# Narrower first score tiles, and chunk-end gate sums with the indicator as the stationary operand, in a two-layer hybrid encoder on one Trainium2 core

## The chip, the cores and the metric

The kernel runs on one core of a Trainium2 chip. The core has a matrix engine (PE in the profile, with its weight loads listed apart as PEld), a vector engine (DVE), an activation engine (ACT), a general engine (POOL), and a queue engine (SP) that mostly starts DMA transfers. The metric is device time in microseconds for one execution. Before the change the median of three runs is 1642.15 us (1640.87 to 1643.2). Lower is better.

A matmul on PE has a stationary operand, which is loaded into the array first (a LDWEIGHTS record in the profile), and a moving operand that is streamed through it. In `nc.tensor.matmul(out, a, b)` the second argument is the stationary one and the third the moving one. Where the text says "128 columns" of a matmul, it means the columns of the moving operand.

## The reference, cut to what matters

```python
D_MODEL = 2048; SEQ = 512; DEPTH = 2; CHUNK = 64
GLA_HEADS = 4; GLA_DK = 128; GLA_DV = 256; ATT_HEADS = 8; ATT_HD = 128

def gla_chunk_causal(q, k, v, log_a):
    L = jnp.cumsum(log_a.reshape(B, nc, CHUNK, H, DK), axis=2)
    L_end = L[:, :, -1]                        # sum of the log gates of a chunk
    k_dec = kf * jnp.exp(L_end[:, :, None] - L)
    U = jnp.einsum('bnchk,bnchv->bnhkv', k_dec, vf)
    A = jnp.exp(L_end)                         # decay of the state over a chunk
    # S_c = A_c * S_{c-1} + U_c, every frame of chunk c reads S_c

def chunk_band_attention(q, k, v, rel_bias):
    # queries of chunk c attend to chunks c-8..c, plus a relative bias, softmax

def hybrid_layer(x, ...):
    z = rmsnorm(x, g_pre) @ w_in               # one projection, columns split into groups
    log_a = log_sigmoid(ga @ w_alpha + b_alpha) / 16
    o_gla = rmsnorm(gla_chunk_causal(gq, gk, gv, log_a)) * silu(gg)
    o_att = rmsnorm(chunk_band_attention(aq, ak, av, rel_bias)) * silu(ag)
    return x + rmsnorm(concatenate([o_gla, o_att]) @ w_out, g_post)
```

There are 512 tokens, so 8 chunks of 64 tokens, and 4 tiles of 128 tokens. A query tile i (128 tokens) attends to the keys 0 to 128(i+1), since 9 chunks reach back to the start of the sequence. `A` has one number for each layer, head, key feature and chunk: 4 x 128 x 8 per layer.

## The kernel before, in words

Nearly all the work is two large matrix products per layer (the input and the output projection), cut into blocks of 512 columns (`std_gemm`, line 340) and, for pairs of blocks, into seven products of halves in place of eight (`fast_gemm`, lines 416 and 426). Every operand is split into a high and a low float32 part (`float32r`, the type `F32R` in the code), and three products of parts are accumulated: high by high, high by low, low by high. The weights come from HBM by SP's queue, ACT makes the high part (line 217), DVE the low part (line 222), and PE multiplies.

Everything else (norms, gates, attention, gated linear attention) is written as Python generators, "tasks". After each block of projection matmuls a pacing object advances the first tasks by a few steps, so that their instructions stand between those of the projection. The framework then orders the instructions of each engine by its own estimate of a timeline when the program is built; each engine executes its own list strictly in that order.

Two tasks are touched by the change.

- **Attention scores** (`Head.scores`, lines 863 to 888). For each head and query tile i three float32r matmuls (lines 871 to 873) give 128 queries by `n` keys in one PSUM tile, with the queries as stationary operand. `n` is `max(lk, 256)` with `lk = (i + 1) * P`, P = 128. For i = 0 that is 256 keys, though only the first 128 are read afterwards. 8 heads by 2 layers by 3 matmuls are 48 such matmuls.
- **Decay of the gates** (`forget_gate_decay`, from line 754). For each of four token tiles t, `ps_g` is the gate's projection (line 781), three activations and one DVE operation make the log gates `la` (128 tokens by 512 features), and they are split into `lah` and `lal`. `finish_tile` sums them: lines 769 and 770 are two float32r matmuls with the fixed matrix `later` as stationary operand, and line 772 makes the chunk sums. There, `la` itself (plain float32) is stationary, 128 by 128 for each head, and the moving operand is `chunk_ind`, two columns that hold 1/16 for the tokens of the first and the second chunk of the tile. The result stands with features on partitions, 2 columns per tile and head, 32 columns in all (`ps_end`). At the end one ACT instruction (line 803) writes `a_end`, the exponential of these 32 columns. `a_end` is read much later, when the states are accumulated (line 1101, first at 605.7 us), and the flag `fgate["done"]` lets the key block's evacuation begin.

A plain float32 matmul leaves two records in the profile, a float32r matmul one. Transposes (line 893) are matmuls of plain float32 with an identity as moving operand and leave one record.

Of the kernel before, what the change touches and what calls it, by code (L numbers as in the profile page):

```python
# [7 lines left out]
F32 = mybir.dt.float32  # L8
F32R = mybir.dt.float32r
BF16 = mybir.dt.bfloat16  # L10
AF = mybir.ActivationFunctionType
# [4 lines left out]
P = 128  # L16
# [4 lines left out]
NT = S // P  # L21
# [13 lines left out]
def hybrid_trunk(  # L35
# [13 lines left out]
    nc = tc.nc  # L49
    cpool = ctx.enter_context(tc.tile_pool(name="cpool", bufs=1))  # L50
# [15 lines left out]
    def nm(s):  # L66
        serial[0] += 1
        return f"{s}_{serial[0]}"

    def slot(tag, shape, dtype=F32):  # L70
        return slots.tile([P] + shape, dtype, tag=tag, name=nm(tag))
# [4 lines left out]
    def t2(shape=(512,), dtype=F32):  # L76
        return tmp.tile([P] + list(shape), dtype, tag="t2", name=nm("t2"))
# [7 lines left out]
    def sm(cols, tag="sm", bufs=None):  # L85
        return small.tile([P, cols], F32, tag=tag, name=nm(tag), **({"bufs": bufs} if bufs else {}))

    def aux():
        return ps_ax.tile([P, 512], F32, tag="ax", name=nm("ax"))
# [14 lines left out]
    def flat(t):  # L104
        return t.bitcast(F32).rearrange("p a b -> p (a b)")

    def split(hi, lo, src):
        nc.scalar.copy(hi, src)  # L108
        nc.vector.tensor_tensor(out=lo, in0=src, in1=hi.bitcast(F32), op=ALU.subtract)
# [9 lines left out]
    ident = cst[:, 0:P]  # L119
    chunk_ind = cst[:, 2 * P : 2 * P + 2]  # L120
    ones = cst[:, 2 * P + 2 : 3 * P + 2]
    mhalf = cpool.tile([P, 4], F32, tag="mhalf", name="mhalf")
    eps = cpool.tile([P, 1], F32, tag="eps", name="eps")
    later = cpool.tile([P, P], F32R, tag="later", name="later")

    CO = (0, 4, 1, 5, 2, 6, 3, 7)
    OO = (5, 4, 7, 6, 2, 3, 0, 1)
# [400 lines left out]
    def neg_inv_rms(l, t):  # L528
        return norm[l][:, 1, t : t + 1]

    def rms(l, t):
        return norm[l][:, 2, t : t + 1]
# [141 lines left out]
    nc.gpsimd.memset(mhalf, -0.5)  # L674
    nc.gpsimd.memset(eps, EPS)
    nc.vector.tensor_copy(later, cst[:, P : 2 * P])

    fg_weights = {}

# [26 lines left out]
    def layer(l):  # L706
# [22 lines left out]
        a_end = sm(32, "a_end", 2)  # L729
# [28 lines left out]
        def forget_gate_decay():  # L758
            fac = slot("g8", [2, 512], F32R)
            nc.sync.dma_start(flat(fac)[0:98], fac_d[l][0:98])  # L760
            wal, gaT = fac[0:98, 0, :], fac[0:98, 1, :]
            yield
            ps_end = aux()

            def finish_tile(t, la, lah, lal):
                if t % 2 == 0:
                    decay.append(slot(f"g{9 + t // 2}", [2, 512]))
                ps_d = aux()
                nc.tensor.matmul(ps_d, later, lah, start=True, stop=False)
                nc.tensor.matmul(ps_d, later, lal, start=False, stop=True)  # L770
                for h in range(4):
                    nc.tensor.matmul(
                        ps_end[:, h * 8 + 2 * t : h * 8 + 2 * t + 2], la[:, h * P : (h + 1) * P], chunk_ind,
                        start=True, stop=True,
                    )
                nc.scalar.activation(decay[t // 2][:, t % 2, :], ps_d, AF.Exp)

            pend = []
            for t in range(NT):
                ps_g = aux()  # L780
                nc.tensor.matmul(ps_g, gaT[:, t * P : (t + 1) * P], wal, start=True, stop=True)
                e = t2()
                nc.scalar.activation(e, ps_g, AF.Abs)
                nc.scalar.activation(e, e, AF.Exp, scale=-1.0)
                nc.scalar.activation(e, e, AF.Ln, bias=ones[:, 0:1])
                la = t2()
                nc.vector.scalar_tensor_tensor(
                    out=la, in0=ps_g, scalar=0.0, in1=e, op0=ALU.min, op1=ALU.subtract
                )
                yield  # L790
                lah, lal = t2(dtype=F32R), t2(dtype=F32R)
                split(lah, lal, la)
                yield
                yield
                pend.append((t, la, lah, lal))
                if t:
                    finish_tile(*pend.pop(0))
                    yield
            for _ in range(4):
                yield  # L800
            finish_tile(*pend.pop(0))
            yield
            nc.scalar.activation(a_end, ps_end[:, 0:32], AF.Exp)
            fgate["done"] = True
            yield

# [39 lines left out]
        def load_bias(n):  # L846
            if n >= 8:
                return
            b = tmp.tile([P, 512], F32, tag="bias", name=nm("bias"), bufs=2)
            src = rel[l, HEADS[n]]  # L850
            nc.sync.dma_start(b, bass.AP(tensor=src.tensor, offset=src.offset + 127, ap=[[639, P], [1, 512]]))
            nc.vector.memset(b[0:64, 448:512], MASKED)
            biases[HEADS[n]] = b
# [4 lines left out]
        class Head:  # L858
# [6 lines left out]

            def scores(self, i):
                lk = (i + 1) * P
                n = max(lk, 256)
                t = slice(i * P, (i + 1) * P)
                ps = aux()  # L870
                nc.tensor.matmul(ps[:, :n], self.qh[:, t], self.kh[:, :n], start=True, stop=False)  # L871
                nc.tensor.matmul(ps[:, :n], self.qh[:, t], self.kl[:, :n], start=False, stop=False)  # L872
                nc.tensor.matmul(ps[:, :n], self.ql[:, t], self.kh[:, :n], start=False, stop=True)  # L873
                pr = self.prob[i] = t2((lk,))
                nc.scalar.activation(pr, biases[self.hd][:, 512 - lk : 512], AF.Copy, scale=rms(l, i))
                nmx = sm(1)
                nc.vector.tensor_tensor_reduce(
                    out=pr, in0=ps[:, :lk], in1=pr, op0=ALU.add, op1=ALU.min,
                    scale=neg_inv_rms(l, i), scalar=-NEG, accum_out=nmx,
                )  # L880
                nc.scalar.activation(pr, pr, AF.Exp, bias=nmx, scale=-1.0, accum_out=self.lsum[:, i : i + 1])
                if i == 0:
                    self.el = sm(4)
                    nc.vector.scalar_tensor_tensor(
                        out=self.el, in0=self.lsum, scalar=EPS, in1=self.lsum, op0=ALU.mult, op1=ALU.mult
                    )
                    load_bias(HEADS.index(self.hd) + 2)
# [129 lines left out]

        until(lambda: 0 in heads_done)
        tasks.insert(0, forget_gate_decay())
        kdh, kdl, gqT = [], [], []  # L1020

# [378 lines left out]
```

## Time and profile before

| | |
|---|---|
| median of three runs | 1642.15 us (1640.87 to 1643.2) |
| the profiled execution | 1640.27 us, of which the span from first to last instruction is 1638.3 us |
| granted TensorE clock | 0.999 |
| PE busy | 1628.6 us (99% of the span), 9030 matmul records |
| DVE busy | 1227.9 us (75%) |
| ACT busy | 903.3 us (55%) |
| POOL busy | 161.9 us (10%) |
| DMA | 469.59 MB, mean 287 GB/s |

A matmul's duration in the profile is longer than the time that it costs, because matmuls overlap: the 512-column ones are listed with some 390 ns each but start every 0.227 us. What one costs is therefore read from the distance between starts, or from the chain of waits, whose pieces do not overlap. The page's busy shares do not tell it.

### The profile page before, as it was taken

Reading aid. Unit: us, or ns where it says so; the run is one execution under the profiler, and the core shown is the slowest. Engines: PE = TensorE matmul, PEld = TensorE weight load, DVE = VectorE, ACT = ScalarE, POOL = GpSimd, SP = SyncE. Lnnn points to the kernel's source line nnn. Section 1 sums busy time; section 2 is a strip of 40 time slices with the busy share of each in tenths; the row PEclk is TensorE's granted clock in tenths of the full one; section 3 lists DMA queues with packets and bytes.
Section 4 is the critical chain, followed back from the end, with each engine's and each line's share of the span. In section 5 each row is a group of like instructions: output and inputs, shape, how many; then the busy total and the mean of one; then the engine's idle time right before and its main releaser. Section 6 shows DMA issues by size and latency. Waiting matters only on the chain.

```text
span 1638.3 us, 24908 instructions
## 1 busy us (share of the span) xinstructions
PE 1628.6 (99%) x9030; PEld 1397.8 (85%) x9030; DVE 1227.9 (75%) x1583; ACT 903.3 (55%) x1514; POOL 161.9 (10%) x258
## 2 busy tenths in 40 slices
PE   9999999999999999999999999999999999999998
PEld 7888889999988877788888888899999888777886
DVE  7567776877877886778886676768778778766887
ACT  8444544556666644545784445445556766445543
POOL 1210000000101101310122000000001001013100
PEclk9999999999999999999999999999999999999999
DMA  9979786858858696898789697968588576968986
GB/s 374 362 281 327 274 316 228 298 184 312 288 185 291 209 376 235 300 365 314 279 297 385 238 327 270 322 219 302 190 307 281 196 275 231 358 225 331 369 306 238
DMA packets 150778, 469.59 MB, mean 287 GB/s; under 512 B 16428, under 2 KB 35892, under 8 KB 150656
## 3 DMA queue, kind: packets, MB, share of 16 engines
q1 hardware_dynamic: 128064, 389.69, 67.9%
q0 software_dynamic: 22016, 77.37, 12.1%
q8 instruction: 71, 1.16, 0.3%
q10 hardware_dynamic: 576, 0.95, 0.2%
q14 instruction: 51, 0.42, 0.1%
HBM read 395.83 MB, written 71.06 MB: 285 GB/s over the span
## 4 chain that ended last, share of the span: by engine, by line
PE 98%; DMA 1%; DVE 0%; issue 0%; ACT 0%; DVEq 0%; POOLq 0%
PE mm L426 46%; PE mm L340 21%; PE mm L416 20%; PE ax L910 2%; PE ax L1080 1%; PE ax L426 1%; PE ax L893 1%; PE ax L1114 1%; PE ax L741 1%; DMA t<-fg 1%; PE ax L873 1%; PE ax L872 1%; PE ax L871 1%; PE ax L1142 0%; PE ax L941 0%; PE ax L568 0%
## 5 line engine op out<-in xcount | busy, mean ns | idle before, releaser
L426 PE MATMUL mm<-wh,sa 128*128 128x512 f32 x1536 | 484.5, 391 | 0.1
L217 ACT CAST wh<-raw 128x1024 fp32r<-128x1024 f32 x255 | 268.7, 1055 | 252.6 <-PE mm L426 119.5
L222 DVE TENSOR_TENSOR wl<-raw,wh 128x1024 fp32r<-128x1024 f32 (+1 forms) x257 | 312.4, 1217 | 118.8 <-PE mm L426 37.2
L217 ACT CAST wh<-H 128x1024 fp32r<-128x1024 f32 x224 | 235.3, 1053 | 219.9 <-PE mm L426 117.6
L222 DVE TENSOR_TENSOR wl<-H,wh 128x1024 fp32r<-128x1024 f32 x224 | 273.3, 1222 | 109.0 <-PE mm L426 49.4
L426 PEld LDWEIGHTS mm<-wh,sa 128*128 128x128 f32 x1536 | 288.1, 188 | 61.6 <-issue 2.3
L426 PE MATMUL mm<-wl,sa 128*128 128x512 f32 x768 | 300.3, 391 | 0.0
L416 PE MATMUL mm<-sa,wh 128*128 128x256 f32 x1280 | 237.1, 285 | 0.0
L416 PEld LDWEIGHTS mm<-sa,wh 128*128 128x128 f32 x1280 | 199.9, 191 | 0.3
L426 PE MATMUL mm<-wh,a 128*128 128x512 f32 x576 | 186.5, 393 | 0.0
L416 PE MATMUL mm<-sa,wl 128*128 128x256 f32 x640 | 180.6, 283 | 0.0
L426 PEld LDWEIGHTS mm<-wl,sa 128*128 128x128 f32 x768 | 144.3, 188 | 29.1
L340 PE MATMUL mm<-wh,a 128*128 128x512 f32 x512 | 166.9, 393 | 0.0
L206 DVE TENSOR_TENSOR H<-H,raw 128x1024 f32<-128x1024 f32 x120 | 145.9, 1220 | 3.7 <-DMA raw<-in_w_dram 2.0
L464 POOL TENSOR_TENSOR sm<-sm,mhalf 128x4 f32<-128x4 f32 (+2 forms) x40 | 53.0, 1325 | 770.5 <-DVE sm L926 542.5
L426 PEld LDWEIGHTS mm<-wh,a 128*128 128x128 f32 x576 | 107.9, 188 | 23.1 <-issue 0.8
L416 PEld LDWEIGHTS mm<-sa,wl 128*128 128x128 f32 x640 | 122.3, 191 | 0.1
L340 PEld LDWEIGHTS mm<-wh,a 128*128 128x128 f32 x512 | 95.9, 188 | 21.2 <-ACT a L108 0.6
L426 PE MATMUL mm<-wl,a 128*128 128x512 f32 x288 | 113.4, 394 | 0.0
L340 PE MATMUL mm<-wl,a 128*128 128x512 f32 x256 | 100.3, 393 | 0.3 <-DVE wl L222 0.3
L416 PE MATMUL mm<-a,wh 128*128 128x256 f32 x512 | 94.7, 285 | 0.0
L340 PE MATMUL mm<-wh,sa 128*128 128x512 f32 x256 | 86.0, 394 | 0.0
(203 smaller groups left out, 2337.3 us busy)
## 6 DMA issues: line engine op xcount, KB each, us to landing
raw<-in_w_dram SPq DMA_DIRECT2D x319, 512.0 KB, 5.7
sa<-S SPq DMA_DIRECT2D x192, 512.0 KB, 4.8
H<-in_w_dram SPq DMA_DIRECT2D x56, 512.0 KB, 4.7
sa<-A SPq DMA_DIRECT2D x48, 512.0 KB, 6.4
S<-g POOLq DMA_DIRECT2D x32, 512.0 KB, 7.2
oS<-g POOLq DMA_DIRECT2D x32, 512.0 KB, 6.5
sa<-oS SPq DMA_DIRECT2D x32, 512.0 KB, 4.7
sg<-t POOLq DMA_DIRECT2D x32, 256.0 KB, 5.9
```

What stands on the lines that cost most here:

```text
L206: nc.vector.tensor_tensor(out=h, in0=h, in1=r, op=ALU.add)
L217: last_cast[0] = nc.scalar.copy(self.wh, src).ins
L222: last_low[0] = nc.vector.tensor_tensor(out=self.wl[:, kk, :], in0=self.src[:, kk, :], in1=self.wh[:, kk, :].bitcast(F32), op=ALU.subtract ...
L340: mm = nc.tensor.matmul(pss[o], a[:, part, t], rhs[:, kk, :], start=(i == 0 and kk == 0 and m == 0), stop=(i == n - 1 and kk == 1 and m == 2),
L416: nc.tensor.matmul(dst, lhs[:, kk, f], a[:, part, tok], start=(fresh and kk == 0 and m == 0 and ft % 2 == 0), stop=(c == c_last and kk == ...
L426: nc.tensor.matmul(out_ps[t], a[:, part, tok], rhs[:, kk, :], start=(fresh and kk == 0 and m == 0), stop=(c == c_last and kk == 1 and m == ...
L464: return nc.gpsimd.tensor_tensor(out=out_r, in0=v, in1=mhalf[:, : v.shape[-1]], op=ALU.pow).ins
L741: nc.tensor.matmul(ps[0:96, half * 256 : (half + 1) * 256], wga[kt // 10][:, kt % 10, :], op[:, i, (kt % 2) * 256 : (kt % 2 + 1) * 256], s ...
L871: nc.tensor.matmul(ps[:, :n], self.qh[:, t], self.kh[:, :n], start=True, stop=False)
L872: nc.tensor.matmul(ps[:, :n], self.qh[:, t], self.kl[:, :n], start=False, stop=False)
L873: nc.tensor.matmul(ps[:, :n], self.ql[:, t], self.kh[:, :n], start=False, stop=True)
L910: nc.tensor.matmul(o, self.pt[i][:, j * P : (j + 1) * P], av[hd // 4, j // 2][:, j % 2, (hd % 4) * P : (hd % 4 + 1) * P], start=(j == 0), ...
```

## The change

Two edits, both in the places named above.

The first lets `n` be `lk`, so that the scores of the first query tile are computed over 128 keys.

The second replaces the chunk sums. A new constant `chunk_sel` (128 by 4 by 8, float32r) holds, for token tile t, the two indicator columns at places 2t and 2t+1 of eight columns, and zeros elsewhere. It is made at the start by one POOL memset and four DVE casts. For each t, two float32r matmuls with `chunk_sel[:, t, :]` (8 columns) as stationary operand and `lah` and `lal` (512 columns) as moving operand accumulate into the same 8 partitions by 512 features of `ps_end`, over all four t. At the end ACT copies these 8 rows to SBUF (`ends`), four PE transposes turn them to 128 features by 8 chunks per head in a new PSUM tile, and ACT's exponential reads that tile.

```diff
+    chunk_sel = cpool.tile([P, NT, 8], F32R, tag="chunk_sel", name="chunk_sel")
...
     nc.vector.tensor_copy(later, cst[:, P : 2 * P])
+    nc.gpsimd.memset(chunk_sel.bitcast(F32), 0.0)
+    for t in range(NT):
+        nc.vector.tensor_copy(chunk_sel[:, t, 2 * t : 2 * t + 2], chunk_ind)
...
                 nc.tensor.matmul(ps_d, later, lah, start=True, stop=False)
                 nc.tensor.matmul(ps_d, later, lal, start=False, stop=True)
-                for h in range(4):
+                for i, part in enumerate((lah, lal)):
                     nc.tensor.matmul(
-                        ps_end[:, h * 8 + 2 * t : h * 8 + 2 * t + 2], la[:, h * P : (h + 1) * P], chunk_ind,
-                        start=True, stop=True,
+                        ps_end[0:8, :], chunk_sel[:, t, :], part,
+                        start=(t == 0 and i == 0), stop=(t == NT - 1 and i == 1),
                     )
...
-            nc.scalar.activation(a_end, ps_end[:, 0:32], AF.Exp)
+            ends = t2()
+            nc.scalar.copy(ends[0:8], ps_end[0:8, :])
+            yield
+            ps = aux()
+            for h in range(4):
+                nc.tensor.transpose(ps[:, h * 8 : (h + 1) * 8], ends[0:8, h * P : (h + 1) * P], ident[0:8, 0:8])
+            nc.scalar.activation(a_end, ps[:, 0:32], AF.Exp)
...
-                n = max(lk, 256)
+                n = lk
```

In the changed program the line numbers of everything behind the first edit are 1 to 10 higher. The names below are those of the built programs: `mm` are the projection's PSUM tiles, `ax` the other PSUM tiles, `wh` and `wl` the weights' high and low parts, `sa` the activations' parts, `t` temporaries.

The first place is on PE, where the first token tile's sums are made. Before:

```order
L426 MATMUL mm_4718<-wh_4735,sa_4695 128x512
L769 MATMUL ax_4836<-t_832_4773,later 128x512
L772 MATMUL ax_4743<-cst,t_827_4750 128x2 x4
L426 MATMUL mm_4718<-wl_4764,sa_4695 128x512
L770 MATMUL ax_4836<-t_833_4774,later 128x512
L426 MATMUL mm_4718<-wh_4735,sa_4695 128x512
```

And now:

```order
L427 MATMUL mm_4724<-wh_4741,sa_4701 128x512
L773 MATMUL ax_4842<-t_832_4779,later 128x512
L776 MATMUL ax_4749<-t_832_4779,chunk_sel 8x512
L427 MATMUL mm_4724<-wl_4770,sa_4701 128x512
...
L427 MATMUL mm_4724<-wh_4773,sa_4745 128x512
L774 MATMUL ax_4842<-t_833_4780,later 128x512
L776 MATMUL ax_4749<-t_833_4780,chunk_sel 8x512
L427 MATMUL mm_4725<-wh_4773,sa_4745 128x512
```

The four matmuls of two columns are gone; one matmul of 512 columns stands behind each of the two that use `later`, and the second pair stands seven projection matmuls further back.

The second place is on PE, behind the last token tile's sums, where the turned rows are made. Now:

```order
L776 MATMUL ax_4749<-t_871_4933,chunk_sel 8x512
L427 MATMUL mm_4722<-wh_4982,sa_4954 128x512
...
L427 MATMUL mm_4724<-wh_5027,sa_5005 128x512
L812 MATMUL ax_5033<-cst,t_891_5031 128x8 x4
L903 MATMUL ax_5059<-cst,t_778_4514 128x128
L881 MATMUL ax_5086<-g_699_4114,g_697_4112 128x128
L882 MATMUL ax_5086<-g_700_4115,g_697_4112 128x128
L883 MATMUL ax_5086<-g_699_4114,g_698_4113 128x128
L427 MATMUL mm_4725<-wh_5027,sa_5005 128x512
```

Between the last sum and the four transposes (line 812) stand 27 projection matmuls of 512 columns. Behind the transposes stand one head's transpose (L903, line 893 before) and one head's three scores of the first query tile, now 128x128.

The third place is ACT's list at the same point of the program. Before:

```order
L217 CAST wh_5003<-H_4649 128x1024
L776 ACTIVATE g_878_4958<-ax_4959 128x512
L217 CAST wh_5029<-raw_4950 128x1024
L803 ACTIVATE a_end_248<-ax_4743 128x32
L776 ACTIVATE g_878_4958<-ax_5007 128x512
```

And now:

```order
L218 CAST wh_5053<-raw_4984 128x1024
L780 ACTIVATE g_878_4960<-ax_5007 128x512
L808 COPY t_891_5031<-ax_4749 8x512
L218 CAST wh_5080<-raw_5055 128x1024
L376 ACTIVATE ev_5122<-mm_4722,norm_208 128x512
L218 CAST wh_5116<-raw_5082 128x1024
L376 ACTIVATE ev_5124<-mm_4723,norm_208 128x512
L813 ACTIVATE a_end_254<-ax_5033 128x32
```

The copy of the eight rows (line 808) stands right behind the last tile's exponential, and the exponential that writes `a_end` stands five instructions later than the copy, behind two weight casts and two evacuations.

## The prediction

> **What bounds the kernel now.** I read the page first: the busy shares, then the chain of waits, then the idle time of the engines that feed PE.
>
> ```profile
> span 1638.3 us, 24908 instructions
> PE 1628.6 (99%) x9030; PEld 1397.8 (85%) x9030; DVE 1227.9 (75%) x1583; ACT 903.3 (55%) x1514; POOL 161.9 (10%) x258
> PE 98%; DMA 1%; DVE 0%; issue 0%; ACT 0%; DVEq 0%; POOLq 0%
> L217 ACT CAST wh<-raw 128x1024 fp32r<-128x1024 f32 x255 | 268.7, 1055 | 252.6 <-PE mm L426 119.5
> ```
>
> A busy PE alone proves little, since overlapping matmuls look busy. The chain is the stronger view: 98% of the span is PE following PE. The last row gives the direction of the waiting: the cast that makes the weights' high part stood idle 252.6 us ahead of its 255 instructions, most of it for PE to free a buffer. The feeders wait for PE, not PE for them. Next I took the stretches in which the two edits stand.
>
> ```profile
> core 0: us, PE busy (x) PEld busy (x) DVE busy (x) ACT busy (x) POOL busy (x), PEclk, DMA share, GB/s
> 0.00:20.00 20.00, 18.82 (x72) 12.65 (x73) 14.80 (x29) 15.27 (x26) 1.19 (x12) 1.00 0.91 338
> 320.00:440.00 120.00, 120.00 (x991) 119.11 (x990) 94.61 (x162) 76.55 (x163) 11.39 (x12) 1.00 0.72 249
> 440.00:500.00 60.00, 60.00 (x312) 51.13 (x312) 46.18 (x59) 38.92 (x66) 1.03 (x1) 1.00 0.67 236
> ```
>
> The attention runs from 320 us and the gates' decay lies in 440 to 500 (the second layer repeats both). PE has no gap there at the full clock, DVE has 14 us free of 60, ACT 21 us, and the DMA engines a third of their time. So the time of the kernel is the sum of what its PE instructions occupy one after another, and the change is worth what it takes from that sum, unless it makes PE wait.
>
> What an instruction occupies I read from the chain, cut to 440 to 500 us; its columns are the start, the length and the instructions of a piece.
>
> ```profile
> 442.49 0.67 PE ax L910 x6
> 443.16 0.12 PE ax L871
> 443.29 0.12 PE ax L872
> 443.40 0.12 PE ax L873
> ...
> 456.75 0.23 PE ax L769
> 456.98 0.79 PE ax L772 x8
> 457.77 0.34 PE mm L426
> 458.11 0.23 PE ax L770
> 458.33 4.99 PE mm L426 x22
> ...
> 465.39 0.34 PE ax L772 x4
> 465.73 0.35 PE ax L769
> 466.07 0.34 PE ax L772 x4
> 466.41 0.34 PE ax L770
> ...
> 492.11 0.76 PE ax L893 x7
> 492.87 5.49 PE mm L426 x24
> ```
>
> And the groups by shape, for the counts and the shapes (the middle number is the listed mean in ns):
>
> ```profile
> L910 PE MATMUL ax<-g,t 128*128 128x128 f32 x320 | 45.9, 274 | 0.0
> L893 PE MATMUL ax<-cst,t 128*128 128x128 f32 x160 | 26.9, 272 | 0.0
> L871 PE MATMUL ax<-g,g 128*128 128x256 f32 x32 | 9.6, 301 | 0.0
> L772 PE MATMUL ax<-cst,t 128*128 128x2 f32 x64 | 7.8, 235 | 0.0
> ```
>
> **The price list.** A 512-column float32r matmul: 4.99 / 22 = 0.227 us. A 256-column one (L871 to L873): 0.12 us. A record of the two-column matmul (L772): eight occupy 0.79 us, and the matmul behind them takes 0.34 instead of 0.23, so 0.79 + 0.11 = 0.90 us per token tile, 0.112 per record. Where the eight are split into four and four, it is 0.34 + 0.12 + 0.34 + 0.11 = 0.91 us (the excess of L769 and L770 over 0.23 counted), the same. A transpose record of 128 columns (L893): 0.76 / 7 = 0.11 us. A plain float32 record of 128 columns (L910): 0.67 / 6 = 0.11 us, two of them per matmul, 0.22.
>
> The reading that carries the forecast is in these four: a record with two columns costs as much as one with 128. The streamed columns do not set the price there. What two, 128-column transposes and 128-column float32 records have in common is that each loads 128 stationary columns. So I take 0.11 us as the floor of any matmul with a 128-column stationary operand, and 256 columns at 0.12 as only just above it.
>
> **Chunk sums, removed.** 64 records (32 matmuls, two records each) at 0.112 us: 8 tiles by 0.90 = 7.2 us off the path.
>
> **Chunk sums, added.** 4 tiles by 2 parts by 2 layers = 16 float32r matmuls of 512 columns. The nearest row is L769, which streams the same `lah`: 0.23 us. 16 x 0.227 = 3.6 us. The stationary operand has 8 columns here, which can only shorten its load, and that load is hidden behind the 0.227 us anyway; I see no reason for a price on either side of this.
>
> **Turning, added.** Four transposes per layer, 8 in all. No row has 8 stationary partitions and 8 moving columns. From above they cost what L893 does, 0.11; from below nothing, if so small a load and so few columns hid behind the matmul ahead. The stationary operand still has 128 columns, like L772's, so I take 0.11: 8 x 0.11 = 0.9 us; the lower end would give 0. The Trainium skill speaks to the point no row shows: "TensorE: Matmul & The Clock Gate", section "LDWEIGHTS", says a load's time goes by the stationary columns (P / 1.2 ns) and not by the rows; by it 8 rows cost the same 107 ns as 128, as I took it.
>
> **Scores, narrowed.** 48 of the 96 matmuls in the 256-column rows of L871, L872 and L873 (32 each; the other half is i = 1) go from 256 to 128 columns. No float32r matmul of fewer than 256 columns is in this trace, so I bound it. From below: if only columns counted, 0.12 - 128 x 0.107/256 = 0.067 us, a gain of 48 x 0.053 = 2.6 us. From above: if it went as the plain float32 matmul of 128 columns, 0.22 us, a loss of 48 x 0.10 = 4.8 us. I take the floor of 0.11, because the load is the same 128 by 128 as in the rows that show the floor: a gain of 48 x 0.01 = 0.5 us.
>
> **What could wait.** The transposes wait for ACT's copy, and PE executes in order, so all the projection stands behind them. Cover: 27 matmuls by 0.227 = 6.1 us between the last sum and the first transpose. In that time ACT has one exponential and the copy to do; their nearest rows are these (groups by shape on ACT).
>
> ```profile
> L776 ACT ACTIVATE g<-ax 128x512 f32<-128x512 f32 x8 | 4.8, 596 | 1.5 <-PE ax L770 1.2
> L896 ACT COPY t<-ax 128x512 f32<-128x512 f32 x16 | 9.3, 581 | 0.0
> ```
>
> 0.6 + 0.6 = 1.2 us against 6.1, so I cost it at nothing; without the cover it would be 1.2 us per layer. `a_end` is ready a few us later than at 481 us, and its first reader starts at 605.7 us: nothing.
>
> The four small casts of `chunk_sel` stand on DVE at the start, where PE is just being filled. DVE's timeline there:
>
> ```profile
> 7.76 0.22 DVE L676 CAST later<-cst 128x128 fp32r<-128x128 f32 x1
> 8.04 0.35 DVE L583 TENSOR_SCALAR H<-H,gcol 128x256 f32<-128x256 f32 x1
> 8.59 0.69 DVE L109 TENSOR_TENSOR g<-g,g 128x512 fp32r<-128x512 f32 x1 [0.19 <-ACT g L108]
> 9.65 0.69 DVE L109 TENSOR_TENSOR a<-H,a 128x512 fp32r<-128x512 f32 x1 [0.37 <-ACT a L108]
> ```
>
> From above a cast costs the 0.22 of the wide one, four 0.9 us; by the small ones' spacing it is nearer 0.07 to 0.1, four 0.3 to 0.4. DVE idles 0.19 and 0.37 us for ACT right behind, which takes 0.3 to 0.4 up; I put 0.1 us on PE, between 0 and 0.5. The POOL memset lies on an engine that is 10% busy.
>
> **Sum.** -7.2 + 3.6 + 0.9 - 0.5 + 0.1 = -3.1 us. The profiled execution took 1640.27 us (span 1638.3, 2.0 around it), so it would take 1637.2; it stands 1.9 below the median of the runs, and the median goes from 1642.15 to **1639.1 us**, 0.19% down. What a measurement of this kernel can tell from no change is about 0.2%, or 3.3 us, so the forecast lies right at that edge.
>
> **The rivals.**
>
> *Columns alone.* The narrow scores cost 0.067 us and not 0.11, because a load can overlap the matmul ahead when that matmul is float32r too. Against it: L910 and L893 at 0.11. For it: these are all plain float32, of which the trace shows two records per matmul, so float32r might load faster. Then -2.6 in place of -0.5: -5.2 us, 1637.0. The Trainium skill, "TensorE: Matmul & The Clock Gate", section "Back-to-back issue gap", goes this way: about 81 ns per matmul at 128 columns in a stream, by which the 48 would save 1.9 us, an estimate, and the sum would be -4.5. The same section's 131 ns at 512 columns is not borne out by the 0.227 here, so I do not lean on it.
>
> *Narrow float32r is slow.* Below 256 columns the matmul takes as many passes as plain float32. The place is L871 to L873 of the first query tile, the price 0.22 each, +4.8 in place of -0.5. Sum: -7.2 + 3.6 + 0.9 + 4.8 + 0.1 = +2.2 us, 1644.4, slower than before. It decides from a price of 0.12 + 2.6 / 48 = 0.174 us per narrow matmul on (the other terms give -2.6). For it: the trace has no float32r matmul under 256 columns, so nothing rules it out. Against: the float32r operands leave one record at every width from 256 to 512, and what costs 0.22 in the trace are two records of plain float32. The Trainium skill, "FP8 and Floating Point Precision", section "TensorE Precision Notes", gives four passes to true FP32 and separates from it the reading that truncates; it names no width.
>
> *The freed time is not had.* PE's list is shortened by 3 us, but the stage is then held by its feeders, or the reordered DVE and ACT lists in 440 to 500 us make PE wait for a weight part or for the copy: -1 to 0 us, 1641.6. For it: the order of DVE's low parts and ACT's casts changes around these tasks. Against: the feeders' idle time is spent waiting for PE, and both have over 14 of 60 us free.
>
> **How the numbers follow.** I give 0.66 to the forecast, 0.12 to columns alone, 0.09 to slow narrow matmuls and 0.13 to the time not had. The forecast's own range is 1637.6 to 1640.6: the terms bounded above, and the scatter of a median of three whose runs lie 2.3 us apart. The range for 8 in 10 reaches to columns alone below and past the time not had above: 1636.8 to 1642.2; the slow narrow matmul is left out. Faster by over 0.2% (below 1638.9): nearly half of the forecast's 0.66, say 0.29, and nearly all of columns alone, 0.41 in all. Slower by over 0.2% (above 1645.4): half of the slow case, since 1644.4 is under that line, 0.04, and 0.02 for a wait that I do not see, 0.06. Within 0.2%: 0.53.
>
> **What would show it.** In the profile after: L776 with 16 records that occupy 0.23 us each in the chain, and no excess behind them; L812 with 8 records near 0.11; the 128x128 rows of L881 to L883 spaced by 0.11 us (0.07 means columns alone, 0.22 the slow case); the stretch from the decay's first sum to the transposes without idle time on PE; and the matmul records down by 40 (64 removed, 24 added). The forecast is wrong if PE shows idle time ahead of L812, or if the narrow scores are off 0.11 by more than 0.05.

## The result, and the profile after

The changed kernel takes 1637.15 us (median of nine runs, 1636.36 to 1640.52), the kernel before 1641.72 us in the same comparison. The ratio is 0.9975, with a 95% interval of 0.9966 to 0.9983: 4.1 us less, between 2.8 and 5.6. The predicted time was 1639.1 us, the range 1636.8 to 1642.2. The profiled executions differ by 3.1 us in their spans, 1638.3 before and 1635.2 after, which is the forecast sum to a tenth. Part of that closeness is luck: two more profiles of the kernel before, shown below, have spans of 1642.1 and 1639.2 us, and with either of them the difference would have been larger.

The page of the changed kernel:

```profile
span 1635.2 us, 24844 instructions
PE 1625.8 (99%) x8990; PEld 1392.6 (85%) x8990; DVE 1228.0 (75%) x1587; ACT 904.6 (55%) x1516; POOL 169.9 (10%) x259
```

There are 40 matmul records fewer (64 gone, 24 new), and PE is as full as before. What the new instructions occupy stands in the chain of waits of the changed kernel, cut to 440 to 500 us (start, length, instructions; L773 and L774 are the matmuls with `later`, L776 the chunk sums, L812 the turning, L903 the heads' transposes):

```profile
459.09 0.24 PE ax L774
459.33 0.24 PE ax L776
459.57 5.04 PE mm L427 x22
...
481.42 0.23 PE ax L776
481.64 6.16 PE mm L427 x27
487.80 0.34 PE ax L812 x4
488.14 0.26 PE ax L903
488.40 0.06 PE ax L881
488.46 0.11 PE ax L882
488.58 0.11 PE ax L883
488.69 4.86 PE mm L427 x21
```

Each chunk-sum matmul occupies 0.23 to 0.24 us, and the 22 projection matmuls behind it take 5.04 us, 0.05 more than 22 of them took before. The four transposes, one more transpose and the three narrow scores end at 488.69: 0.89 us for eight matmuls, 0.11 each on average; the four of line 812 are not told apart from the rest. The 27 projection matmuls ahead of the transposes took 6.16 us, and no wait stands between them and the transposes, so the cover for ACT's copy held.

A narrow score group beside 256-column matmuls, in the changed kernel's PE timeline (start, listed length):

```profile
343.57 0.28 PE L417 MATMUL mm<-a,wl 128*128 128x256 f32 x1
343.69 0.22 PE L881 MATMUL ax<-g,g 128*128 128x128 f32 x1
343.75 0.28 PE L882 MATMUL ax<-g,g 128*128 128x128 f32 x1
343.87 0.27 PE L883 MATMUL ax<-g,g 128*128 128x128 f32 x1
343.98 0.45 PE L417 MATMUL mm<-a,wh 128*128 128x256 f32 x2
344.27 0.28 PE L417 MATMUL mm<-a,wl 128*128 128x256 f32 x1
```

Inside the group the starts are 0.11 to 0.12 us apart (343.75, 343.87, 343.98). The starts of the weight loads (PEld in the same stretch: 343.58, 343.70, 343.81 for the three, 343.92 for the next) are as far apart. The second start is only 0.06 us behind the first, and the matmul behind the group gives that back: the two of them at 343.98 take 0.29 us and not 0.24. From 343.69 to 344.27 there are three narrow and two wide ones: 0.58 - 2 x 0.12 = 0.34, so 0.113 us for a narrow one.

### The profile page after: what moved, and what is told of

It is laid out like the page before. It is cut to its first block, busy times and chain, and to the rows that moved or that the text cites. A ratio compares the mean times of both kernels' runs of the same rounds, so it can differ in the third digit from the quotient of the medians.

```text
span 1635.2 us, 24844 instructions
## 1 busy us (share of the span) xinstructions
PE 1625.8 (99%) x8990; PEld 1392.6 (85%) x8990; DVE 1228.0 (75%) x1587; ACT 904.6 (55%) x1516; POOL 169.9 (10%) x259
## 4 chain that ended last, share of the span: by engine, by line
PE 99%; DMA 0%; DVE 0%; ACT 0%; SPq 0%; DVEq 0%; POOLq 0%; issue 0%
PE mm L427 46%; PE mm L341 22%; PE mm L417 20%; PE ax L920 2%; PE ax L1090 1%; PE ax L427 1%; PE ax L903 1%; PE ax L1124 1%; PE ax L745 1%; PE ax L882 1%; PE ax L883 1%; PE ax L881 1%; PE ax L1152 0%; PE ax L569 0%; PE ax L951 0%; DMA raw<-in_w_dram 0%
## 5 line engine op out<-in xcount | busy, mean ns | idle before, releaser
L465 POOL TENSOR_TENSOR sm<-sm,mhalf 128x4 f32<-128x4 f32 (+2 forms) x40 | 60.6, 1514 | 777.7 <-DVE sm L936 550.8
```

Of the source, the lines that this page charges most:

```text
L465: return nc.gpsimd.tensor_tensor(out=out_r, in0=v, in1=mhalf[:, : v.shape[-1]], op=ALU.pow).ins
```

## The experiments

The forecast gave one reading of four rows (a matmul with 128 stationary columns costs at least 0.11 us, however few columns it streams), and two rivals another. The first runs undo one edit or one part of it, the next measure the price by itself, and the last use it.

### Each edit alone

The first run has the first edit on the kernel before:

```diff
-                n = max(lk, 256)
+                n = lk
```

> The kernel before with the first edit alone (first query tile's scores over 128 keys, chunk sums as before). Theory (a floor of 0.11 us for a matmul with 128 stationary columns): 48 matmuls go from 0.12 to 0.111 us, 0.4 us less than before, so no change that a timing can tell, and starts inside the group 0.11 us apart. Rival (the columns alone set the price, 0.067 us): 2.6 us less, ratio 0.9984. Rival (the rest of the measured gain lies in this edit, since the median fell by 4.6 us and the sum gave 3.1): 1.5 to 2 us less.

Measured: 1641.28 us against 1641.99 before, ratio 0.9995 (0.9985 to 1.0004). No change that can be told; columns alone (0.9984) lies just outside the interval. The third reading, that the unexplained part of the gain is in this edit, would give 0.9988 to 0.9991, which this interval still holds; it is the next run that speaks against it.

The second run has the second edit alone (the changed kernel with `n = max(lk, 256)` put back).

> The kernel before with the second edit alone (chunk indicator stationary, rows turned; scores over 256 keys as before). Theory: 64 records at 0.112 us removed, 16 at 0.235 and 8 transposes added: 2.7 us less than before, ratio 0.9983. Rival (the gain comes from the new order of the other engines and not from PE's sum): clearly off that, nearer 0 or nearer 4.5.

Measured: 1637.15 us against 1641.99, ratio 0.9969 (0.9958 to 0.9981), a gain of 5.1 us, between 3.1 and 6.9. So the second edit carries all of the gain that can be measured, and the 2.7 us that were expected of it lie outside the interval: PE's sum does not account for all of it. The rival's 4.5 us fit, but not its reason alone, since the span shrank by the sum too. The profile shows 40 matmul records fewer, and a span 3.3 us shorter than the first one of the kernel before:

```profile
span 1635.0 us, 24848 instructions
PE 1625.2 (99%) x8990; PEld 1392.8 (85%) x8990; DVE 1228.9 (75%) x1587; ACT 905.2 (55%) x1516; POOL 169.8 (10%) x259
```

Where the other 2 us come from is taken up at the end of this section.

### The roles, or the type?

The second edit does two things: it makes the indicator stationary, and it goes from plain float32 to float32r. This run keeps the second and undoes the first.

```diff
-                for i, part in enumerate((lah, lal)):
-                    nc.tensor.matmul(
-                        ps_end[0:8, :], chunk_sel[:, t, :], part,
-                        start=(t == 0 and i == 0), stop=(t == NT - 1 and i == 1),
-                    )
+                for h in range(4):
+                    for i, part in enumerate((lah, lal)):
+                        nc.tensor.matmul(
+                            ps_end[:, h * 8 + 2 * t : h * 8 + 2 * t + 2], part[:, h * P : (h + 1) * P],
+                            chunk_sel[:, t, 2 * t : 2 * t + 2], start=(i == 0), stop=(i == 1),
+                        )
```

> The changed kernel, but the chunk sums keep the old roles: the log gates are stationary (128 columns), the indicator moves (2 columns), now in float32r as high and low part, so 8 matmuls of one record each per token tile; no copy and no transposes. This separates the exchange of the roles from the exchange of float32 for float32r. Theory (the load of 128 stationary columns is the price, in either type): 64 records at 0.11 us as before, so the gain of the second edit is gone and about 0.4 us of the first is left: 0.4 us less than before. Rival (plain float32 was the price, float32r loads faster): 64 records at 0.067 or less, 3 us or more less than before.

Measured: 1640.83 us, ratio 0.9993 (0.9985 to 1.0002). The gain is gone, as the load of 128 columns would have it, and the rival's 3 us are outside the interval. Its chain (L777 are the two-column float32r matmuls):

```profile
459.12 0.23 PE ax L774
459.35 0.67 PE ax L777 x7
460.03 4.69 PE mm L427 x20
```

Seven records in 0.67 us, and 4.69 us for twenty 512-column matmuls, 0.15 more than 20 x 0.227: 0.82 us for seven, 0.12 each. So float32r with two columns costs what plain float32 did. It is the exchange of the roles that pays, and with it that one matmul serves all four heads.

### The price by itself

Three runs put 144 matmuls more into the changed kernel, in three shapes.

```diff
                 ps = aux()
+                if i == 0:
+                    for _ in range(9):
+                        nc.tensor.matmul(ps[0:q, :n], self.qh[:, 0:q], self.kh[:, :n], start=True, stop=True)
                 nc.tensor.matmul(ps[:, :n], self.qh[:, t], self.kh[:, :n], start=True, stop=False)
```

Here `q` is the stationary and `n` the moving number of columns: 128 and 128, 128 and 64, 32 and 128.

> The changed kernel with nine more matmuls ahead of each first query tile's scores, 144 in all, whose result is overwritten: 128 stationary columns, 128 moving columns, float32r. It measures the disputed price by itself. Theory (floor of the load): 144 by 0.111 us, 16.0 us more than the changed kernel. Rival (columns alone): 144 by 0.067, 9.6 us more. Rival (narrow float32r is slow): 144 by 0.22, 32 us more.

> As the run with 128 by 128, but the 144 added matmuls have 64 moving columns. Theory (floor of the load, moving columns do not count below 256): again 16.0 us more than the changed kernel. Rival (columns alone, 0.04 us): 5.8 us more.

> As the run with 128 by 128, but the 144 added matmuls have 32 stationary columns and 128 moving columns. This separates a floor that is the load of the stationary columns from a floor that any matmul has. Theory (the load of 128 columns is the floor): with a load of a quarter the moving columns decide, 144 by 0.067 us, 9.6 us more than the changed kernel. Rival (a fixed floor per matmul of 0.11 us): 16.0 us more.

| stationary x moving columns | median, us | against the kernel before (interval) | span, us | more than the changed kernel's 1635.2, per matmul |
|---|---|---|---|---|
| 128 x 128 | 1654.02 | 1.0077 (1.0062 to 1.0092) | 1651.9 | 16.7 us, 0.116 us |
| 128 x 64 | 1654.43 | 1.0081 (1.0065 to 1.0098) | 1650.7 | 15.5 us, 0.108 us |
| 32 x 128 | 1646.63 | 1.0034 (1.0021 to 1.0047) | 1644.8 | 9.6 us, 0.067 us |

Six of them in a row in the chain, from the three profiles in the table's order:

```profile
321.62 0.62 PE ax L883 x6
```

```profile
321.02 0.59 PE ax L883 x6
```

```profile
321.68 0.36 PE ax L883 x6
```

The spans hold a little more than the matmuls: beyond the wait at the start, PE waits 1.4, 1.0 and 1.1 us in these three profiles and not at all in the changed kernel's. Without these waits the prices are 0.106, 0.101 and 0.059 us, which agrees with the chain (0.62, 0.59 and 0.36 us for six).

This settles the price of the narrow matmuls with 128 stationary columns. Halving their moving columns changes next to nothing. Cutting the stationary columns to a quarter takes the price from 0.106 to 0.059 us. So the floor of 0.11 goes with the stationary columns: it is not a floor of any matmul, and it does not need plain float32. That narrow float32r is slow, at 0.22, is out: it would have been 32 us. What sets the 0.06 that is left is not shown. The 128 moving columns may decide there, as the prediction's "columns alone" had it at 0.067, but no run has fewer moving columns beside 32 stationary ones; and that the span's 9.6 us met the expected 9.6 is luck, as 1.1 of it are waits. The Trainium skill, "TensorE: Matmul & The Clock Gate", section "LDWEIGHTS", gives the load as stationary columns / 1.2 ns, 107 ns for 128; the 0.101 to 0.106 without the waits, and the 0.108 to 0.116 with them, lie around that.

### Taking the new matmuls away as well

If the time is PE's sum, the 16 new matmuls of 0.235 us are the next 3.8 us. The decay's own matmuls nearly make the chunk sum already: they sum the gates of the tokens behind each token, and the chunk's last token has an empty sum.

```diff
-    later = np.where(same & (i[:, None] > i[None, :]), 1.0 / 16.0, 0.0)
+    later = np.where(same & ((i[:, None] > i[None, :]) | (i[None, :] % 64 == 63)), 1.0 / 16.0, 0.0)
...
-                for i, part in enumerate((lah, lal)):
-                    nc.tensor.matmul(
-                        ps_end[0:8, :], chunk_sel[:, t, :], part,
-                        start=(t == 0 and i == 0), stop=(t == NT - 1 and i == 1),
-                    )
-                nc.scalar.activation(decay[t // 2][:, t % 2, :], ps_d, AF.Exp)
+                nc.scalar.activation(decay[t // 2][:, t % 2, :], ps_d, AF.Exp, scale=not_last)
+                sums = t2()
+                nc.scalar.copy(sums, ps_d)
+                for c in range(2):
+                    nc.scalar.dma_start(ends[2 * t + c : 2 * t + c + 1], sums[64 * c + 63 : 64 * c + 64])
...
-            ends = t2()
-            nc.scalar.copy(ends[0:8], ps_end[0:8, :])
-            yield
+            for _ in range(6):
+                yield
             ps = aux()
```

`not_last` is a new column of the constants, zero for the last token of each chunk and one elsewhere; `ends` is a tile of its own, made at the task's start, and `chunk_sel` is gone. The four transposes and the exponential follow as in the changed kernel.

> The changed kernel with the 16 chunk-sum matmuls taken away: the fixed matrix of the decay gets the whole chunk's sum in the column of each chunk's last token (whose own decay is the exponential of zero), ACT's exponential sets that token's decay to one by a scale of zero, and ACT copies the decay sums to SBUF, from where two rows per token tile go by DMA into the eight rows that are turned. Theory (the kernel's time is PE's sum, other engines have room): 16 matmuls by 0.235 us less than the changed kernel, 3.8 us, so 6.9 to 7.5 us less than before, ratio 0.9956. Rival (ACT, with 8 copies of 0.6 us and 16 DMA issues more, or the DMA, makes PE wait): 0 to 3 us less than the changed kernel, or more time than it.

Measured: 1640.97 us, ratio 0.9995 (0.9986 to 1.0003): none of the 3.8 us, and the changed kernel's own gain lost as well. The profiled execution, 1643.32 us, is the slowest of the eleven. The two largest waits of PE in its profile (engine, line, what it waited for, us in total, times, longest):

```profile
PE ax L877 <- DVE sm L883: 3.5, 2, 1.8
PE ax L899 <- ACT t L887: 1.2, 2, 0.6
```

And by stretches, with the granted clock third from the end:

```profile
505.00:513.00 8.00, 8.00 (x51) 7.17 (x50) 3.16 (x10) 3.76 (x11) 1.64 (x2) 1.00 0.74 253
513.00:516.00 3.00, 1.16 (x8) 0.82 (x6) 1.77 (x7) 3.00 (x13) 1.03 (x1) 1.00 0.32 114
516.00:520.00 4.00, 3.45 (x15) 3.08 (x16) 2.02 (x9) 3.09 (x10) 0.00 (x0) 0.57 0.23 66
```

PE waits for a head's softmax (L883 and L887), which is not what I had named: no wait of PE stands at the transposes, so the copies and the transfers were not late. The place, once in each layer, is where the program must have one of the last attention heads finished (`until(lambda: 6 in heads_done)`) before it can go on. There 47 matmuls, nearly all of the attention, stand without a projection matmul between them, against 32 in the changed kernel. In the first layer the wait costs more than itself, for the clock falls to 0.57 behind it; in the second layer the same waits leave it at 1.00. These waits are 4.7 us in all. PE waits another 3.3 us in four other places of this profile (at 7.5, 323.8, 863.9 and 1338.6 us). My suspicion was the six empty steps that I had put ahead of the transposes: tasks share a number of steps, and each one spent by the decay is one fewer for the attention. The next run takes the steps away and leaves the copies and the DMA; it also issues the transposes later and sets the flag `fgate["done"]` earlier.

```diff
-            for _ in range(6):
-                yield
-            ps = aux()
-            for h in range(4):
-                nc.tensor.transpose(ps[:, h * 8 : (h + 1) * 8], ends[0:8, h * P : (h + 1) * P], ident[0:8, 0:8])
-            nc.scalar.activation(a_end, ps[:, 0:32], AF.Exp)
+            def turn_ends():
+                ps = aux()
+                for h in range(4):
+                    nc.tensor.transpose(ps[:, h * 8 : (h + 1) * 8], ends[0:8, h * P : (h + 1) * P], ident[0:8, 0:8])
+                nc.scalar.activation(a_end, ps[:, 0:32], AF.Exp)
+
+            delayed.append([14, turn_ends])
             fgate["done"] = True
```

> The run with the sums taken from the decay's own matmuls, with the same ACT copies and DMA transfers, but the four transposes are issued 14 steps later without taking steps of their own, and the six empty steps of the decay's task are gone; the flag that lets the key block's evacuation begin is set at once. In that run PE waited 1.8 us twice for DVE and 0.6 us twice for ACT around 513 us and 1331 us, in a stretch where 47 attention matmuls stand without a projection matmul between them (32 in the changed kernel). Theory (the empty steps pushed the attention back and left it without projection work beside it): those waits are gone, and the gain of the 16 removed matmuls appears: 3.8 us less than the changed kernel, 7 to 8 us less than the kernel before. Rival (ACT's eight copies and its DMA issues make PE wait): still within 1 us of the kernel before.

Measured: 1632.94 us against 1640.91, ratio 0.9949 (0.9935 to 0.9963), by which it is 8.4 us less than before (6.1 to 10.7); its median is 4.2 us below the changed kernel's 1637.15. It is the fastest of the versions. The two waits are gone, and so are the other four places; one wait of 0.9 us is left, for a transfer. The page and the chain at the same place, where L807 are the transposes:

```profile
span 1632.3 us, 24843 instructions
PE 1621.9 (99%) x8974; PEld 1391.6 (85%) x8974; DVE 1227.2 (75%) x1583; ACT 907.7 (56%) x1522; POOL 168.6 (10%) x258
```

```profile
500.48 0.34 PE ax L807 x4
500.82 2.92 PE mm L428 x12
...
514.20 0.44 PE ax L948 x4
514.63 1.56 PE ax L917 x14
516.20 0.07 issue
516.27 1.06 PE ax L1033 x8
```

ACT's eight copies and sixteen transfers, which both versions have, cost nothing that is seen here; with the number of matmuls in that stretch back at 32, the whole gain is there. The run takes away the empty steps, the early place of the transposes and the late flag together. That it was the empty steps follows from the program, in which each advance goes to the first task alone, and not from a run that changes them alone.

### The part of the gain that PE's sum does not hold

The median fell by more than the 3.1 us of the sum. Three more executions were profiled, two of the kernel before and one of the changed one, with no edit.

> The kernel before once more, for its profile alone. The first profiled execution stood 1.9 us below its median, and the median fell by 4.6 us where PE's sum fell by 3.1. If the rest is waiting that comes and goes with the transfers, this profile has a longer span than 1638.3 us and the difference lies in waits of PE for DVE, ACT or DMA (at the start, near 711 us, at the end), with PE's own pieces the same. If the rest is in PE's own work, the added waits do not account for it.

> As the look before, a third sample of the same kernel: span and PE's waits are to agree with each other within 0.5 us, sample by sample, if waits carry the scatter.

> The changed kernel once more, for its profile alone. If its waits are rarer by nature, PE's waits beyond the start stay under 0.5 us here as in its first profile (1635.2 us); if it was luck, they come and go as in the kernel before.

Measured: 1644.12 us (span 1642.1), 1641.26 (1639.2) and 1636.69 (1634.8). The number of matmul records is the same in all profiles of one kernel. PE's waits beyond the start are 0.35, 2.75 and 1.01 us in the three profiles of the kernel before, and none in the two of the changed kernel. The third span is thereby explained within 0.3 us. The second is 3.8 us longer than the first and its waits only 2.4, which misses the 0.5 us that were expected; the rest is the clock, which stood at half speed for 3 us behind the waits, some 1.5 us (an estimate). With the waits and that estimate taken off, the three spans come to 1638.0, 1637.9 and 1638.2 us, and the changed kernel's are 1635.2 and 1634.8: 2.7 to 3.4 us less, about the sum of 3.1. The scatter above it is waiting, and what the waiting does to the clock.

Most of the waits lie in one place, the start of the output projection of the first layer (0.97 us of the second profile stand elsewhere, at 865 us). By stretches, first the kernel before in its second profile, then the first edit alone, then the changed kernel in its second profile (PE is the second number, then PEld, DVE and ACT; the DMA share is the last but one):

```profile
700.00:710.00 10.00, 10.00 (x45) 8.29 (x45) 3.10 (x4) 1.18 (x2) 0.04 (x1) 1.00 1.04 386
710.00:720.00 10.00, 8.21 (x28) 6.01 (x27) 8.86 (x12) 7.52 (x11) 2.14 (x4) 0.83 1.03 408
```

```profile
700.00:710.00 10.00, 10.00 (x46) 8.29 (x45) 2.45 (x2) 1.06 (x1) 0.53 (x1) 1.00 1.04 388
710.00:720.00 10.00, 7.49 (x32) 5.57 (x32) 9.78 (x13) 7.84 (x12) 1.61 (x3) 1.00 1.03 398
```

```profile
700.00:710.00 10.00, 9.95 (x44) 7.96 (x43) 5.44 (x7) 3.56 (x5) 0.54 (x1) 1.00 1.04 402
710.00:720.00 10.00, 10.00 (x45) 8.26 (x44) 10.00 (x13) 7.49 (x12) 1.60 (x3) 1.00 1.00 386
```

From 700 to 720 us the DMA engines have no time free. In the second profile of the kernel before PE waits 1.8 us:

```profile
711.38 0.73 PE L340 MATMUL mm<-wh,a 128*128 128x512 f32 x2 [0.95 <-ACT wh L217]
712.95 0.77 PE L340 MATMUL mm<-wl,a 128*128 128x512 f32 x1 [0.83 <-DVE wl L222]
713.51 1.05 PE L340 MATMUL mm<-wh,a 128*128 128x512 f32 x2
714.37 0.63 PE L340 MATMUL mm<-wl,a 128*128 128x512 f32 x1
```

and behind that wait its matmuls start 0.43 us apart until the clock is back. What PE waits for are weight parts, but the weights' transfers are not what is late: the weight casts start without a wait as soon as ACT comes to them (at 710.28 and 712.32 us). ACT and DVE do little from 700 to 710 us because ACT's list has a cast of another operand ahead of the next weight cast, and DVE's part of that operand (L621) waits for a tile of the gated linear attention's output that comes back from HBM (`t<-fg`). In the chain of waits its transfer takes 14.01 us:

```profile
694.85 14.01 DMA t<-fg
...
708.96 0.70 DVE t L621
...
709.68 0.63 ACT g L108
...
712.95 4.60 PE mm L340 x12
```

ACT's line for that cast, with its wait, in the second profile of the kernel before and in the first of the changed kernel:

```profile
709.68 0.62 ACT L108 CAST g<-t 128x512 fp32r<-128x512 f32 x1 [8.82 <-DVE t L621]
```

```profile
706.67 0.62 ACT L108 CAST g<-t 128x512 fp32r<-128x512 f32 x1 [6.63 <-DVE t L622]
```

All thirteen profiles fit one rule: PE has some 6.8 to 7 us of work in hand there, and waits for about as long as ACT's wait goes beyond that.

| ACT's wait for that operand, us | PE's waits behind it, us | profiles |
|---|---|---|
| 5.58 to 6.80 | none | changed kernel (6.63, 6.80), second edit alone, old roles in float32r, both versions without chunk-sum matmuls, 128 x 64 added |
| 6.95, 7.10, 7.35 | 0.20, 0.35, 0.60 | 128 x 128 added, kernel before (first), 32 x 128 added |
| 8.03, 8.82, 9.54 | 1.01, 1.78, 2.50 | kernel before (third, second), first edit alone |

So the second edit also spares waits that the kernel before has in all three profiles. But the changed kernel stands close to the edge: the waits come back in two of the three runs that add matmuls to it, and one of its own nine executions took 1640.52 us, for which there is no profile. Why that tile lands later in the kernel before is not shown: the changed order of SP's transfers (a bias, a gate and an operand load each moved by a few places in the stretch of the decay) and the earlier arrival of PE are both possible. It does not follow from an earlier PE alone, since ACT's wait is short in the float32r run with the old roles too (6.69) while its PE comes hardly earlier.

## Why the prediction was right, point by point

- **What bounds the kernel.** Right in the main. What was added to PE's sum or taken from it was paid or had in full, the 144 added matmuls too, but up to 2.8 us of waiting came on top in the kernel before, and 8.1 in the first version without chunk-sum matmuls. The row that gave the direction of the waiting shows 119.5 of 252.6 us for PE, less than half; with the waits for the other two projection lines, L340 and L416, it is 204.5, so the reading holds.
- **Chunk sums, removed: 7.2 us, and added: 3.6 us.** Right. The 16 new ones occupy 0.235 us and not 0.227, 3.8 us in all. The old roles in float32r cost 0.12 for each matmul, as the records did before.
- **Turning, added: 0.9 us.** Right as far as it can be read: 0.11 on average in a group of eight matmuls, four of them these. ACT's copy was covered, as worked out.
- **Scores, narrowed: 0.5 us less.** Right in its mechanism: 0.113 us in the profile, and the added-matmul runs show that the stationary columns set it. The gain of this edit is too small to be measured, 0.9995 with one in the interval. "Columns alone" was refuted by the runs with 128 and 64 columns, "narrow float32r is slow" by the run with 128; something near the price that "columns alone" named, 0.06 us, is met where the stationary operand is narrow.
- **The start: 0.1 us.** The four casts took 0.37 us on DVE at 8.1 us, and no wait of PE at the start grew so far that the spans show it.
- **The sum, -3.1 us, and the median, 1639.1.** The spans of the two profiled executions differ by exactly that, since the first profile of the kernel before happened to hold only 0.35 us of waits. The measured ratio gives 4.1 us with 2.8 to 5.6, which holds the sum. The median came out 1.9 us lower than forecast, 0.4 of it because the kernel before came out at 1641.72 us and not at 1642.15. The step that failed is the one from the profiled execution to the median: I set the 1.9 us between them down to scatter that the change would carry along unchanged. The further profiles show that this scatter is mostly PE's waiting near 711 us, and neither profile of the changed kernel has it. So 1.5 of the 4.6 us by which the medians differ were forecast by no term; that part was luck.
- **"The freed time is not had".** This rival did not occur here, but something like it befell the first version without chunk-sum matmuls, at another place and with another cause than the prediction named: not the decay's own stretch, but the end of the attention.

## What to carry to other kernels

Price a matmul by both of its operands: with 128 stationary columns it cost 0.11 us here with 2, 64 or 128 streamed columns, so in this kernel the wide operand belonged on the moving side and the narrow one on the stationary side. Where PE is full, a saving in its sum is had; but work that is spread by counted steps shares those steps, and the version with six idle ones lost more than the 16 matmuls saved. When PE waits for a weight part, follow the wait to its start: here it was another operand's transfer, which stood ahead in ACT's list. Before a forecast for a median is made from one profiled execution, ask which waits that execution did not have.

## What the runs showed of the hardware that I had not expected

A wait of PE of under 2 us can cost nearly as much again behind it, or nothing. In the second profile of the kernel before, two waits of 0.95 and 0.83 us were followed by a granted clock of 0.50 from 713 to 716 us:

```profile
711.00:713.00 2.00, 0.79 (x3) 0.35 (x3) 1.97 (x4) 2.00 (x4) 0.54 (x1) 1.00 1.03 401
713.00:716.00 3.00, 3.00 (x7) 2.40 (x8) 3.00 (x5) 2.78 (x4) 1.07 (x2) 0.50 1.04 399
```

Yet waits of 1.65 and 0.85 us at the same place, in the run with the first edit alone, left the clock at 1.00. The first version without chunk-sum matmuls has both outcomes in one execution: waits of 1.76 and 0.62 us near 515 us were followed by a clock of 0.57 from 516 to 520 us, and the same two waits near 1333 us left it at 1.00. So it does not go by the length of the waits alone. The Trainium skill, "TensorE: Matmul & The Clock Gate", section "What's actually happening", says that activity is watched in a free-running window, so that the moment of the wait would matter; these cases agree with that, but no run here moves a wait against the window. The same section has the clock fall after an idle window of about 3.4 us, and here it fell with no single wait longer than 1.76 us.
